# Bias frames built later in program order, and the attention's first loads issued in a forced order

## The chip, the cores and the metric

One core of a Trainium2 chip runs the whole program in one launch. The metric is the device time of one execution in microseconds (us). The core has five instruction streams that each run in order: TensorE (PE, with its weight loads PEld), VectorE (DVE), ScalarE (ACT), GpSimd (POOL) and SyncE (SP, which here only issues DMAs). POOL issues DMAs too. All DMAs share the core's 16 DMA engines.

## What is computed

One layer of a transformer-like backbone over 1024 latent tokens (a 16 x 64 grid) and 256 context tokens, width 1024, fp32. One input projection feeds eight attention heads of size 64 and a long-convolution group of 512 channels; both are normalised, projected out together, and a gated feed-forward layer follows.

```python
def _layer(x, mods, attend, ...):
    h = _rmsnorm(x, norm1_g) * (1.0 + sc1) + sh1
    proj = h @ w_in
    q, k, v = _heads(...), _heads(...), _heads(...)
    hy = _dwconv3(proj[..., 3 * ATTN_WIDTH:], hy_conv_w, hy_conv_b)
    a = attend(q, k, v)                       # latent: neighbourhood attention
    hyo = _hyena(hy, k_f, filt_bias)          # two FFT convolutions with implicit filters
    merged = jnp.concatenate([_rmsnorm(a, ...), _rmsnorm(hyo, ...)], axis=-1)
    x = x + g1 * (merged @ w_out)
    ...                                       # conv feed-forward layer
# neighbourhood attention, per head: an 8 x 16 window with a learned relative bias, plus all context keys
bias = rpb[:, dr[:, None, :, None], dc[None, :, None, :]]
s_loc = jnp.where(col_in, einsum(qg, k_band) * scale + bias, NEG)
s_ctx = einsum(qg, k_ctx) * scale
p = softmax(concatenate([s_loc, s_ctx], -1))
o = einsum(p_loc, v_band) + einsum(p_ctx, v_ctx)
```

## The kernel before

The program is written as straight Python; a list scheduler then sets the order of each engine's stream, from the written order, from priorities and from what it thinks is ready. `tc.issue_after(x)` forces the DMAs (or other instructions) written under it behind instruction x. Stages, in order of time:

- **Projections.** After the first normalisation, `hy_chunk` (L653 and following) makes the long convolution's inputs and `qkv(j, which)` makes Q, K and V of head pair j, all with three-part fp32 matmuls into the banks `psp` (`mm3`, L116 to L118). Results go to DRAM scratch `qd`, `kd`, `vd`. The implicit filters (`filters`, L375 to L489) run beside them and write their spectra to `Kd`, `Kc`.
- **Bias frames.** `rpb_frames(t, var)` (L549 to L558) makes on POOL, for each of three column variants, a frame of the relative bias: a memset, 16 small DMAs, a copy, and a DMA to DRAM scratch `rpw`. Its tile borrows the buffer `fo` of the hyena chunks.
- **Chain.** `chain(j)` is the long convolution of channel group j (five of them, in two interleaved lanes): forward DFT on PE (L805), twiddles on ACT and DVE (L817 to L819), butterflies on DVE (L826 to L831), product with the spectrum `K` loaded from `Kd` on SP (L840 to L847; one buffer `K` per lane), the inverse (L852 to L864, L877), and the gates (L882 to L890). Its inputs `s` are loaded from `lxd` on SP (L791), its result goes to `hyd` (L895, L898). The first phases start in the projections and the rest are interleaved with the attention.
- **Attention.** `attend(p_)` for head pairs 0 to 3. Scores go to `psS` on PE (L1058); DVE adds the bias from `tb0`, `tb1`, `tb2` and takes the maximum (L1079, L1086, L1089); ACT takes exponentials (L1092, L1093); PE transposes (L1102, `psX`), ACT and DVE copy (`pt`, L1006, L1008), PE multiplies with V (L1016, `psav`), and DVE scales into `at` (L1129, L1149). Of all its loads POOL is the issuer: `q` and `k` (L972, L974), `vs` (L1044, L1046: V and cached V), and 16 DMAs of 32 KB for each of the three bias tables of a pair (`bias_load`, L967, from `rpw`). Before pair 0, POOL also fills the three tables with the mask value (L979) and zeroes the borders of the eight probability tiles `Pl` (L984, L985).
- **Output projection** (`wor` loads L1195, splits L1187 and L1188, `token_scales` L1212 to L1226, then matmuls into `psd`), **feed-forward**, final norm. The nine `wor` loads can start only when the chain's pool is given back, which is when its last `hyd` store has landed.

The attention's tiles lie where the projection's operands and weights lay, so each first write waits until the old reader is done. `tb0`, `q0` and `k0` lie in space that is free earlier than that of `Pl`, `tb1` and `tb2`.

Of the kernel before, what the change touches and what calls it, by code (L numbers as in the profile page):

```python
# [11 lines left out]
F32 = mybir.dt.float32  # L12
# [7 lines left out]
P = 128  # L20
# [4 lines left out]
NH, DH = 8, 64  # L25
# [4 lines left out]
NEG = -1e30  # L30
# [47 lines left out]
def build(tc, I, O, dbg=None, upto=99):  # L78
    nc = tc.nc
    V, A, G, T, Q = nc.vector, nc.scalar, nc.gpsimd, nc.tensor, nc.sync  # L80
    dbg = dbg or {}
    top = ExitStack()
    with top:
        _build(nc, tc, top, V, A, G, T, Q, I, O, dbg, upto)


def _build(nc, tc, top, V, A, G, T, Q, I, O, dbg, upto):
    def pool(es, name, bufs=1, **kw):
        return es.enter_context(tc.tile_pool(name=name, bufs=bufs, **kw))
# [51 lines left out]
    def tw_ctx(h):  # L141
# [33 lines left out]
    ld = [("norm1_g", 0, 0, 8), ("norm2_g", 0, 8, 8), ("grp_norm_g", 0, 16, 8), ("hy_conv_w", 0, 40, 36),  # L175
          ("hy_conv_b", 0, 76, 12)]
# [105 lines left out]
    def ft(shape, tag, dt=F32, bufs=1):  # L282
        return fp.tile(shape, dt, tag=tag, name=tag, bufs=bufs)
# [216 lines left out]
    with ies:  # L500
# [3 lines left out]
        for gi, (s, col, tl) in enumerate(groups):  # L504
            xs = []
            for i in tl:
                src, row, _ = tiles[i]
                x = wp.tile([P, D], F32, tag="wada", name="x", bufs=4) if gi in XW else \
# [21 lines left out]
            n = P * len(tl)  # L530
# [19 lines left out]
    def rpb_frames(t, var):  # L550
        f, g = t[:, 0:480], t[:, 512:992]
        G.memset(f, NEG)
        fv = f.rearrange("p (r c) -> p r c", c=32)
        for cq in range(16):
            a = (8 + max(cq - 8, 0), cq, min(cq, 8))[var]
            G.dma_start(out=fv[cq * 8:cq * 8 + 8, :, a:a + 16], in_=I["rpb"][0][:, :, a + 7 - cq:a + 23 - cq])
        G.tensor_copy(g.rearrange("p (u r c) -> p r u c", u=4, r=15), f.rearrange("p (r u c) -> p r u c", u=4, r=15))
        G.dma_start(out=rpw[var].rearrange("q h u x -> (q h) (u x)"), in_=g)  # L558
# [19 lines left out]
    vd = dr.tile([10, P, 512], F32, name="vd")  # L578
# [103 lines left out]
    def qkv(p_, which):  # L682


        w_ = 16 if which == 0 else 8
        t = ip.tile([P, LT], F32, tag=f"cv{turn_('cv')}", name="qkv", bufs=1)

        def sink(ps, c0, n):
            if c0 < LL:
                r0 = c0 // GW  # L690
                src = ps.rearrange("p (r u c) -> p r u c", r=n // GW, c=w_)
                A.copy(t[:, 0:LL].rearrange("p (u r c) -> p r u c", r=16, c=w_)[:, r0:r0 + n // GW], src)
            else:
                A.copy(t[:, LL:LT], ps)

        proj(win[:, :, which * 512 + p_ * P:which * 512 + (p_ + 1) * P], sink, DH ** -0.5 if which == 0 else 1.0)
        if which < 2:
            Q.dma_start(out=(qd, kd)[which][p_, :, 0:LT], in_=t)
        if which == 0:
            return  # L700
        ctx = t[:, LL:LT]
        ps = bk("tB")
        for i in range(2):
            T.transpose(ps[:, i * P:(i + 1) * P], ctx[:, i * P:(i + 1) * P], ident)
        pv = ps[:, 0:256].rearrange("p (n c) -> p n c", n=2)
        so = ip.tile([P, 2, P], F32, tag="st", name="so", bufs=2)
        A.copy(so, pv)
        for i in range(2):
            Q.dma_start(out=O[1 + which][0, 0, 2 * p_:2 * p_ + 2, i * P:(i + 1) * P].rearrange("h t d -> t h d"),
                        in_=so[:, i].rearrange("p (h d) -> p h d", h=2))  # L710
        if which == 2:
            vstore(so, 8, 2, p_)
            for g in range(2):
                ps = bk("tB")
                for i in range(4):
                    T.transpose(ps[:, i * P:(i + 1) * P], t[:, (4 * g + i) * P:(4 * g + i + 1) * P], ident)
                vt = ip.tile([P, 4, P], F32, tag="st", name="vt", bufs=2)
                A.copy(vt, ps.rearrange("p (n c) -> p n c", n=4))
                vstore(vt, 4 * g, 4, p_)
# [4 lines left out]
    def cached(p_):  # L724

        ck = ip.tile([P, 2, P], F32, tag="st", name="ck", bufs=2)
        for h in range(2):
            Q.dma_start(out=ck[:, :, h * DH:(h + 1) * DH],
                        in_=I["cache_ctx_k"][0, 0, 2 * p_ + h].rearrange("(n p) d -> p n d", p=P))
        ps = bk("tB")  # L730
        for i in range(2):
            T.transpose(ps[:, i * P:(i + 1) * P], ck[:, i], ident)
        kt = ip.tile([P, 256], F32, tag="st", name="kt", bufs=2)
        A.copy(kt, ps[:, 0:256])
        Q.dma_start(out=kd[p_, :, LT:], in_=kt)

    for j in range(4):
        for which in range(3):
            hy_chunk(which, j)
            if j + which == 0:  # L740

                t = ft([P, 512], "tm", bufs=2)
# [8 lines left out]
    for j in range(4):  # L751
        for which in range(3):
            if j + which > 0:
                qkv(j, which)
            if j == 0:
                rpb_frames(ip.tile([P, LT], F32, tag="fo", name="rp", bufs=1), which)
        cached(j)
    fes.close()
# [178 lines left out]
    tp = pool(es, "att", reuse_waits="tile")  # L937
# [3 lines left out]
    Pring = [[tp.tile([P, 2, b - a, 16, 8], F32, name=f"Pl{h}{i}") for i, (a, b) in enumerate(BLK)] for h in range(2)]  # L941

    tbs = [None] + [tp.tile([P, NROW * 64], F32, name=f"tb{v}") for v in (1, 2)]
# [12 lines left out]
    blast = [None]  # L956

    def bias_load(p_, var):

        for half in range(2):  # L960
            for rq in range(8):
                r = 8 * half + rq
                r0 = min(max(r - 4, 0), 8)
                nr = HALF_ROWS[half][1]
                a, d = r0 - HALF_ROWS[half][0], r0 - r + 7
                tv = tbs[var][rq * 16:(rq + 1) * 16, HOFF[half]:HOFF[half] + nr * 64].rearrange("q (u x) -> q u x", u=8)
                blast[0] = G.dma_start(out=tv[:, :, a * 8:a * 8 + 64], in_=rpw[  # L967
                    var, :, 2 * p_:2 * p_ + 2, :, d * 8:d * 8 + 64].rearrange("q h u x -> q (h u) x")).ins

    def qkload(p_):  # L970
        q = tp.tile([P, LT], F32, tag=f"q{p_ % 2}", name="q", bufs=1)
        G.dma_start(out=q, in_=qd[p_])  # L972
        k = tp.tile([P, LT + 256], F32, tag=f"k{p_ % 2}", name="k", bufs=1)
        G.dma_start(out=k, in_=kd[p_])  # L974
        return q, k

    first = qkload(0)
    for var in range(3):
        G.memset(tbs[var], NEG)  # L979
        bias_load(0, var)  # L980
        if var == 0:
            for r in Pring:
                for t in r:
                    G.memset(t[:, 0, :, 11:16], 0.0)  # L984
                    G.memset(t[:, 1, :, 0:4], 0.0)  # L985
    blast0 = blast[0]

    sel = tp.tile([P, 4, P], F32, name="sel")
# [49 lines left out]
    def attend(p_):  # L1038

        with tc.issue_after(blast0) if p_ == 1 else ExitStack():  # L1040
            q, k = qkload(p_) if p_ else first
        vs = tp.tile([P, 12, P], F32, tag="vs", name="vs", bufs=2)
        with tc.issue_after(blast0) if p_ == 1 else ExitStack():
            G.dma_start(out=vs[:, 0:10], in_=vd[:, :, p_ * P:(p_ + 1) * P].rearrange("n p x -> p n x"))  # L1044
            for h in range(2):
                G.dma_start(out=vs[:, 10:12, h * DH:(h + 1) * DH],  # L1046
                            in_=I["cache_ctx_v"][0, 0, 2 * p_ + h].rearrange("(n p) d -> p n d", p=P))
        if p_:
            with tc.issue_after(blast0):
                for var in range(3):  # L1050
# [109 lines left out]
    for p_ in range(4):  # L1160
        for n, _ in enumerate(attend(p_)):
            phases(2 - n % 2)
        phases(2)
# [409 lines left out]
    for f in range(NFF):  # L1573
# [8 lines left out]
        t = fpl.tile([P, 2, 2, 256], F32, tag="wt", name="wt", bufs=1)  # L1582
# [191 lines left out]
    for j in range(5):  # L1774
        for i, (g, w) in enumerate(cs):
            dmm(ps[j], g, w, j, False, i == NT - 1)
        t = dp2.tile([P, 512], F32, tag="fx", name="t", bufs=3)
# [44 lines left out]
```

## Time and profile before

| | |
|---|---|
| median of 3 runs | 1855.13 us (1854.43 to 1856.17) |
| the profiled execution's own time | 1859.47 us |
| its span in the trace | 1857.7 us |
| mean granted TensorE clock | 0.962 |
| busy, share of span | PE 93%, PEld 78%, DVE 74%, ACT 48%, POOL 21% |

The profiled execution is 4.3 us (0.23%) longer than the median of the timed runs; the trace's times are its own, from the start of its span. The shares are means over the whole program. The change lies in the stretch from 540 to 880 us, where the projections end, the attention begins, and PE is less busy than in the mean.

### The profile page before, as it was taken

Reading aid. Unit: us, or ns where it says so; the run is one execution under the profiler, and the core shown is the slowest. Engines: PE = TensorE matmul, PEld = TensorE weight load, DVE = VectorE, ACT = ScalarE, POOL = GpSimd, SP = SyncE. Lnnn points to the kernel's source line nnn. Section 1 sums busy time; section 2 is a strip of 40 time slices with the busy share of each in tenths; the row PEclk is TensorE's granted clock in tenths of the full one; section 3 lists DMA queues with packets and bytes.
Section 4 is the critical chain, followed back from the end, with each engine's and each line's share of the span. In section 5 each row is a group of like instructions: output and inputs, shape, how many; then the busy total and the mean of one; then the engine's idle time right before and its main releaser. Section 6 shows DMA issues by size and latency. Waiting matters only on the chain.

```text
span 1857.7 us, 27350 instructions
## 1 busy us (share of the span) xinstructions
PE 1723.9 (93%) x9999; PEld 1453.9 (78%) x9999; DVE 1368.3 (74%) x2166; ACT 892.5 (48%) x1852; POOL 396.3 (21%) x487
## 2 busy tenths in 40 slices
PE   5899999999994689897998899999999999999997
PEld 1688778788783355465886899999999999788786
DVE  4668957861878789873467888889777877556797
ACT  4755545533333576664555444444444444443452
POOL 2366656673018325500110000000000000000001
PEclk7999999999996799898998999999999999999999
DMA  7424354356445323514331444555222122934653
GB/s 265 146 75 142 112 168 131 110 149 211 145 137 160 102 80 102 140 44 144 119 106 65 147 157 146 172 176 165 76 68 67 56 74 96 342 120 136 205 189 130
DMA packets 202438, 249.76 MB, mean 134 GB/s; under 512 B 21922, under 2 KB 147987, under 8 KB 202049
## 3 DMA queue, kind: packets, MB, share of 16 engines
q1 hardware_dynamic: 190360, 230.75, 38.5%
q0 software_dynamic: 10240, 16.46, 3.7%
q8 instruction: 78, 1.28, 0.3%
q10 hardware_dynamic: 1705, 0.82, 0.2%
q14 instruction: 55, 0.45, 0.1%
HBM read 176.75 MB, written 71.20 MB: 133 GB/s over the span
## 4 chain that ended last, share of the span: by engine, by line
PE 54%; DVE 19%; DMA 13%; ACT 5%; issue 5%; POOL 3%; SPq 0%; DVEq 0%; ACTq 0%; POOLq 0%
PE psd L116 5%; PE psd L117 5%; PE psd L118 5%; PE psp L116 4%; PE psp L118 4%; PE psp L117 4%; DMA wt<-in_w_down_dram 3%; PE psa L116 2%; PE psa L117 2%; PE psa L118 2%; DMA tdr<-wt 2%; PE psc L118 2%; PE psc L117 2%; PE psc L116 2%; PE psb L117 1%
## 5 line engine op out<-in xcount | busy, mean ns | idle before, releaser
L116 PE MATMUL psp<-hh,wh 128*128 128x512 f32 (+1 forms) x552 | 200.7, 364 | 1.9 <-ACT wh L121 1.9
L117 PE MATMUL psp<-hl,wh 128*128 128x512 f32 (+1 forms) x552 | 199.0, 361 | 0.0
L118 PE MATMUL psp<-hh,wl 128*128 128x512 f32 (+1 forms) x552 | 199.0, 361 | 0.0
L1737 POOL TENSOR_TENSOR rs<-rs,mhalf 128x1 f32<-128x1 f32 x10 | 7.7, 775 | 816.4 <-DVE rs L1736 816.4
L116 PE MATMUL psa<-T,ws 128*128 128x256 f32 (+1 forms) x528 | 165.8, 314 | 3.8 <-ACT rows L1536 2.7
L117 PE MATMUL psa<-T,ws 128*128 128x256 f32 (+1 forms) x528 | 165.1, 313 | 0.0
L118 PE MATMUL psa<-T,ws 128*128 128x256 f32 (+1 forms) x528 | 164.6, 312 | 0.0
L116 PE MATMUL psd<-wd,gs 128*128 128x512 f32 x360 | 140.7, 392 | 3.6 <-ACT gs L121 3.6
L117 PE MATMUL psd<-wd,gs 128*128 128x512 f32 x360 | 141.0, 392 | 0.0
L118 PE MATMUL psd<-wd,gs 128*128 128x512 f32 x360 | 123.8, 391 | 2.0 <-DVE gs L122 2.0
L116 PEld LDWEIGHTS psp<-hh,wh 128*128 128x128 f32 x552 | 104.9, 190 | 23.2 <-issue 7.4
L118 PEld LDWEIGHTS psp<-hh,wl 128*128 128x128 f32 x552 | 104.6, 189 | 15.3 <-issue 1.2
L117 PEld LDWEIGHTS psp<-hl,wh 128*128 128x128 f32 x552 | 104.9, 190 | 14.0 <-issue 0.4
L116 PE MATMUL psc<-T,ws 128*128 128x384 f32 (+1 forms) x352 | 110.0, 313 | 6.0 <-ACT ws L121 6.0
L967 POOL DMA_DIRECT2D tb<-rpw x192 | 100.3, 530 | 58.0 <-DVE m L1079 24.3
L117 PE MATMUL psc<-T,ws 128*128 128x384 f32 (+1 forms) x352 | 110.1, 313 | 0.0
L118 PE MATMUL psc<-T,ws 128*128 128x384 f32 (+1 forms) x352 | 109.7, 312 | 0.0
L117 PE MATMUL psb<-T,ws 128*128 128x384 f32 (+1 forms) x352 | 109.4, 311 | 0.0
L118 PE MATMUL psb<-T,ws 128*128 128x384 f32 (+1 forms) x352 | 109.4, 311 | 0.0
L116 PE MATMUL psb<-T,ws 128*128 128x384 f32 (+1 forms) x352 | 109.2, 310 | 0.0
L116 PEld LDWEIGHTS psa<-T,ws 128*128 128x128 f32 x528 | 101.3, 192 | 5.5 <-ACT rows L1536 3.9
L117 PEld LDWEIGHTS psa<-T,ws 128*128 128x128 f32 x528 | 101.3, 192 | 0.0
(404 smaller groups left out, 4783.9 us busy)
## 6 DMA issues: line engine op xcount, KB each, us to landing
wada<-in_w_ada_dram SPq DMA_DIRECT2D x48, 512.0 KB
wr<-in_w_up_dram SPq DMA_DIRECT2D x44, 512.0 KB
gr<-gdr SPq DMA_DIRECT2D x44, 320.0 KB
wr<-in_w_in_dram SPq DMA_DIRECT2D x23, 512.0 KB
wt<-in_w_down_dram SPq DMA_DIRECT2D x44, 256.0 KB
tdr<-wt SPq DMA_DIRECT2D x44, 256.0 KB
gdr<-cv SPq DMA_DIRECT2D x22, 512.0 KB
wr<-tdr SPq DMA_DIRECT2D x20, 512.0 KB
```

The source lines that it names most:

```text
L116: T.matmul(out, ah, bh, start=start, stop=False, skip_group_check=True)
L117: T.matmul(out, ah, bl, start=False, stop=False, skip_group_check=True)
L118: T.matmul(out, al, bh, start=False, stop=stop, skip_group_check=True)
L967: blast[0] = G.dma_start(out=tv[:, :, a * 8:a * 8 + 64], in_=rpw[var, :, 2 * p_:2 * p_ + 2, :, d * 8:d * 8 + 64].rearrange("q h u x -> q ( ...
L1737: G.tensor_tensor(rs, rs, mhalf, op=ALU.pow)
```

## The change

Two edits. First, the three `rpb_frames` calls move in written order from head pair 0 to head pair 2 of the `qkv` loop. Second, the loads ahead of the attention get a forced order on POOL: the fill and the 16 loads of `tb0` first, then the three `vs` loads of pair 0 (a new helper `vload`), then, behind `vs`, the border memsets of `Pl`, and the fills and loads of `tb1` and `tb2`. Nothing is computed otherwise; the number of instructions on each engine is the same.

```diff
-            if j == 0:
+            if j == 2:
                 rpb_frames(ip.tile([P, LT], F32, tag="fo", name="rp", bufs=1), which)
...
+    def vload(p_):
+        vs = tp.tile([P, 12, P], F32, tag="vs", name="vs", bufs=2)
+        G.dma_start(out=vs[:, 0:10], in_=vd[:, :, p_ * P:(p_ + 1) * P].rearrange("n p x -> p n x"))
+        for h in range(2):
+            ld = G.dma_start(out=vs[:, 10:12, h * DH:(h + 1) * DH],
+                             in_=I["cache_ctx_v"][0, 0, 2 * p_ + h].rearrange("(n p) d -> p n d", p=P))
+        return vs, ld.ins
...
     first = qkload(0)
-    for var in range(3):
-        G.memset(tbs[var], NEG)
-        bias_load(0, var)
-        if var == 0:
-            for r in Pring:
-                for t in r:
-                    G.memset(t[:, 0, :, 11:16], 0.0)
-                    G.memset(t[:, 1, :, 0:4], 0.0)
+    G.memset(tbs[0], NEG)
+    bias_load(0, 0)
+    with tc.issue_after(blast[0]):
+        vfirst, vlast = vload(0)
+    with tc.issue_after(vlast):
+        for r in Pring:
+            for t in r:
+                G.memset(t[:, 0, :, 11:16], 0.0)
+                G.memset(t[:, 1, :, 0:4], 0.0)
+        for var in (1, 2):
+            G.memset(tbs[var], NEG)
+            with tc.issue_after(blast[0]):
+                bias_load(0, var)
...
-        vs = tp.tile([P, 12, P], F32, tag="vs", name="vs", bufs=2)
         with tc.issue_after(blast0) if p_ == 1 else ExitStack():
-            G.dma_start(out=vs[:, 0:10], in_=vd[:, :, p_ * P:(p_ + 1) * P].rearrange("n p x -> p n x"))
-            for h in range(2):
-                G.dma_start(out=vs[:, 10:12, h * DH:(h + 1) * DH],
-                            in_=I["cache_ctx_v"][0, 0, 2 * p_ + h].rearrange("(n p) d -> p n d", p=P))
+            vs = vload(p_)[0] if p_ else vfirst
```

**POOL, at the frames** (`rp` is a frame's tile, `cs0` and `GO` are the filters' tiles; difference of the order before and after). This is where the moved calls stand in the stream:

```order
 L395 TENSOR_TENSOR cs0_2317<-sd11_2315,sd01_2308 128x512
-L552 MEMSET rp_4064 128x480
-L556 DMA rp_4064<-in_rpb_dram 8x15x16 x13
+L552 MEMSET rp_4714 128x480
+L556 DMA rp_4714<-in_rpb_dram 8x15x16 x13
 L455 TENSOR_TENSOR GO_2068<-GO_2068 128x2x2x128
```

Only the tile's number differs: the frames stand between the same two filter instructions as before, and so do the two other frames. Up to the attention's first loads, the streams of all five engines are the same, instruction by instruction and with the same semaphore waits.

**POOL, ahead of head pair 0, before** (with the semaphores that each waits for):

```order
L979 MEMSET tb0_5857 128x1472 [waits DMAHW1_49,PE_49,Activation_49]
L984 MEMSET Pl00_5833 128x3x40 [waits PE_49]
...
L967 DMA tb0_5857<-rpw_723 16x8x64 [waits Pool_49]
...
L979 MEMSET tb1_5841 128x1472
L979 MEMSET tb2_5842 128x1472
L1044 DMA vs_5944<-vd_728 128x10x128 [waits DMASW5_49]
L1046 DMA vs_5944<-in_cache_ctx_v_dram 128x2x64 [waits DMASW6_49]
```

and after:

```order
L987 MEMSET tb0_5857 128x1472 [waits DMAHW1_49,PE_49,Activation_49]
L967 DMA tb0_5857<-rpw_723 16x8x64 [waits Pool_49]
...
L972 DMA vs_5879<-vd_728 128x10x128 [waits DMASW5_49,PE_49]
L974 DMA vs_5879<-in_cache_ctx_v_dram 128x2x64 [waits DMASW6_49]
...
L994 MEMSET Pl00_5833 128x3x40
...
L997 MEMSET tb1_5841 128x1472
L997 MEMSET tb2_5842 128x1472
```

The wait for PE that the first `Pl` memset had is now the first `vs` load's, on the same semaphore value (the last projection matmul into `psp`). The 16 `tb0` loads now stand ahead of that wait, and no instruction was added.

**DVE, at the end of the attention, before** (`L890` is the chain's last instruction on DVE, `L1188` the split of an output weight, `at` the attention's result, `ria` the token scales):

```order
L890 TENSOR_TENSOR s_8075<-s_8075,s_8073 128x2x256
L1139 TENSOR_TENSOR l<-l,l_8098 128x8
L1182 COPY sh_8287<-mods 128x16
L1024 RECIPROCAL lrow_5941<-l 128x4 x2
...
L1188 SCALAR_TENSOR_TENSOR wl_8328<-wor,vec,wh_8327 128x512
L1149 TENSOR_TENSOR at_5828<-psav,bs 128x2x16x16
L1220 TENSOR_SCALAR ria<-psX 128x2
```

and after:

```order
L890 TENSOR_TENSOR s_8075<-s_8075,s_8073 128x2x256
L1159 TENSOR_TENSOR at_5828<-psav,bs 128x2x16x16
L1020 COPY pt<-psX 128x512
...
L1198 SCALAR_TENSOR_TENSOR wl_8304<-wor,vec,wh_8303 128x1024
L1159 TENSOR_TENSOR at_5828<-psav,bs 128x2x16x16
L1230 TENSOR_SCALAR ria<-psX 128x2
```

The scheduler interleaves chain and attention differently from the second score block of pair 0 on, on PE, DVE and ACT. At the end, 134 attention matmuls stood on PE behind the chain's last matmul before, and 86 do now. Eight of the nine weight splits stood ahead of the attention's last write to `at` before; four do now.

## Rows read from the trace of the kernel before

**Rows 1.** By stretch: length, busy PE, PEld, DVE, ACT, POOL; clock, DMA share, GB/s

```profile
560.00:600.00 40.00, 20.50 (x68) 14.91 (x68) 33.51 (x58) 16.33 (x56) 33.84 (x72) 0.63 0.58 153
...
620.00:834.00 214.00, 188.79 (x1133) 115.53 (x1131) 176.79 (x391) 136.58 (x439) 73.82 (x138) 0.95 0.31 82
834.00:878.00 44.00, 34.38 (x213) 23.36 (x213) 17.16 (x28) 21.88 (x40) 2.37 (x2) 0.88 0.39 122
```

**Rows 2.** Chain that ended last, 538 to 660: start, us, what

```profile
562.24 8.32 POOL tb L967 x16
...
573.49 8.39 DMA vs<-vd
...
582.16 6.13 DMA tb<-rpw
...
602.58 7.93 DMA K<-Kd
```

**Rows 3.** Timeline of DVE: start, us, instruction, [idle before <-releaser]

```profile
585.75 0.48 DVE L819 SCALAR_TENSOR_TENSOR s<-pscA,tw,t 128x256 f32<-128x256 f32 x1 [3.58 <-ACT t L818]
...
597.77 0.42 DVE L1079 CUSTOM_DVE_ANT_0 Pl<-psS,tb 128x264 f32<-128x264 f32 x1
...
605.69 1.21 DVE L1086 TENSOR_REDUCE n<-psS 128x4 f32<-128x1024 f32 x1
610.60 1.23 DVE L844 TENSOR_TENSOR s<-s,K 128x1024 f32<-128x1024 f32 x1 [3.69 <-DMA K<-Kd]
```

**Rows 4.** Timeline of POOL ahead of head pair 0

```profile
544.20 1.33 POOL L979 MEMSET tb<- 128x1472 f32 x1 [3.60 <-PE pstB L704]
560.26 0.20 POOL L984 MEMSET Pl<- 128x120 f32 x1 [14.73 <-PE psp L118]
...
562.18 8.38 POOL L967 DMA_DIRECT2D tb<-rpw  x16
...
573.49 0.98 POOL L1044 DMA_DIRECT2D vs<-vd  x1
574.46 1.44 POOL L1046 DMA_DIRECT2D vs<-in_cache_ctx_v_dram  x2
...
582.16 4.17 POOL L967 DMA_DIRECT2D tb<-rpw  x8 [3.65 <-DMA vs<-vd]
588.58 9.89 POOL L967 DMA_DIRECT2D tb<-rpw  x19 [2.25 <-DMA tb<-rpw]
598.46 0.57 POOL L972 DMA_DIRECT2D q<-qd  x1
```

**Rows 5.** Chain that ended last, 480 to 700: an earlier load of K

```profile
502.56 3.73 DMA K<-Kd
```

**Rows 6.** Timelines of SP and of PE at one load of s

```profile
574.54 0.37 SPq L791 DMA_DIRECT2D s<-lxd  x1
...
582.72 6.25 PE L805 MATMUL pscA<-s,dftf 128*128 128x256 f32 x16 [9.09 <-DMA s<-lxd]
```

**Rows 7.** Timeline at the end of the attention: PE, DVE and SP

```profile
829.28 1.89 PE L877 MATMUL pscA<-s,idft 128*128 128x256 f32 x8
839.59 0.65 PE L1016 MATMUL psav<-pt,vs 128*64 128x256 f32 x4
840.17 0.66 PE L1102 MATMUL psX<-ident,Pl 128*128 128x128 f32 x4
877.16 0.77 PE L116 MATMUL psd<-w,ar 128*128 128x512 f32 x1
...
833.27 0.68 DVE L890 TENSOR_TENSOR s<-s,s 128x512 f32<-128x512 f32 x1
862.14 0.74 DVE L1188 SCALAR_TENSOR_TENSOR wl<-wor,vec,wh 128x512 fp32r<-128x512 f32 x1
864.68 0.69 DVE L1149 TENSOR_TENSOR at<-psav,bs 128x512 f32<-128x512 f32 x1 [1.79 <-ACT bs L1033]
...
836.83 26.41 SPq L1195 DMA_DIRECT2D wor<-in_w_out_dram  x9
```

## The prediction

> **What bounds the kernel now.** I read the busy time by stretch first, since the shares of the whole program say nothing about the place of the change. From 560 to 600 us, where the attention starts, no engine is full: DVE is busy 33.5 of 40 us, PE 20.5 at a granted clock of 0.63, POOL 33.8. From 620 to 834 us PE is busy 188.8 and DVE 176.8 of 214 us, so both are close to the limit. In the last stretch, 834 to 878, DVE is busy 17.2 of 44 us: the work waits on itself there [rows 1]. Outside 540 to 880 us the change alters nothing that I can find, apart from one swap of two neighbouring DMAs on SP in the feed-forward.
>
> Next I read the chain of waits. It goes through POOL: 16 loads of `tb0` (8.32 us), the landing of `vs` (8.39), the landing of a bias load (6.13) [rows 2]. Taken at its word, 22.8 us of POOL's loading lie on the path. The timeline of DVE says otherwise. The first instruction that needs `tb0` is L1079 at 597.77, and it shows no idle time ahead of it: DVE came to it straight from the chain's butterflies [rows 3]. The last `tb0` load was issued by 570.56 (562.18 + 8.38) [rows 4], 27 us earlier. The chain view followed a wait for many semaphores and picked the wrong one. So the tables of pair 0 are not late, and what counts is only the idle time that DVE and PE do show: 3.58 us of DVE ahead of 585.75, where PE had waited 9.09 us for a load of `s`, and 3.69 us of DVE ahead of 610.60, waiting for `K` [rows 3, 6].
>
> **The frames.** The first edit moves nothing. The order shows the frames between the same filter instructions, with the same waits, on POOL and on all other engines. Cost 0, with no range.
>
> **POOL ahead of pair 0.** Before, `tb0` is filled at 544.20, then POOL stands 14.73 us behind the first `Pl` memset until the last projection matmul ends at 560.2. Then come memsets, 16 loads, memsets, `vs` at 573.49, and 32 loads with 5.90 us of waits between them (3.65 for `vs`, 2.25 for a bias load), until `q` of pair 1 is issued at 598.46 [rows 4]. After the change the 16 loads (8.38 us) fill the 14.73 us hole: they run from 545.5 to about 554. Then `vs` waits, since it took over the wait for PE, until 560.2, and its three issues take 2.4 us (0.98 + 1.44). Sixteen border memsets cost about 2.4 us (thirteen took 560.26 to 562.18, less than 0.15 us each), two fills 2 x 1.33, 32 loads 32 x 0.524 = 16.8 us. That is 560.2 + 2.4 + 2.4 + 2.7 + 16.8 = 584.5 for `q` of pair 1 if the loads find no wait, and 590.4 if they find all the 5.90 us again. So POOL runs 8 to 14 us ahead. By itself this is worth nothing, since nothing waited for the tables.
>
> **What it is worth (term 1).** The load of `K` issued at 602.58 took 7.93 us to land [rows 2]. An earlier one took 3.73 [rows 5]. Between 598.46 and 602 POOL had issued `q`, `k` and `vs` of pair 1 in one burst [rows 4], so the slow one shared the DMA engines with it. When the burst is issued at 584.5 to 590.4 instead, it has landed before 602.58 even if it takes the 8.4 us that `vs` took [rows 2]. `K` then lands at 602.58 + 3.73 = 606.3; DVE is busy until 605.69 + 1.21 = 606.9, and the 3.69 us of idle time are gone. ACT's exponentials of pair 0 come behind that DVE work, so they move too. I take the whole 3.69 us. Lower bound of the gain 0, if the 16 loads of `tb0` for pair 1, which may now follow at once, slow `K` just as much.
>
> **Term 2, the load of `s` at 574.54** [rows 6]. `vs` leaves its window (it was issued at 573.49), but more bias loads enter it: before, POOL was still at the memsets until 573.49, after it issues a bias load every 0.52 us from about 567.7. The Trainium skill, page DMA: Bandwidth & Descriptors, section Issuing engines are not separate DMA queues, says that DMAs of all issuers run on the same 16 DMA engines and interleave; the trace agrees at the `K` load (7.93 us beside 3.73). By that rule the bias loads from POOL take from this load about what `vs` gives back. Gain bounds: 3.58 us (all of DVE's idle time) and -2 us (7.93 - 3.73 = 4.2 is the price of a full burst, and the bias loads come half as dense). I take 0.
>
> **Term 3, the end of the attention.** The scheduler, which thinks the tables come earlier, now places attention ahead of chain work. Total work is equal, but the tail differs. Before, the chain's last DVE instruction ends at C = 833.95, the first output matmul `psd` starts at 877.16, 43.2 us later; 134 attention matmuls stood behind the chain, and attention's last write to `at` began at 864.68 [rows 7]. Now 86 stand behind it. Then attention ends about 86/134 of (865.4 - 834.0 = 31.4 us), 20.2 us, after the new C', and the first `psd` follows by the old distance of 877.2 - 865.4 = 11.8: C' + 32.0. The other condition is the weight splits: the nine `wor` loads start only behind C, at 836.83, and the eighth split ends at 862.9, C + 28.9 [rows 7]; the token scales now stand behind it on DVE, and take some 3 us more: C' + 32. Both give 11.2 us less than 43.2. But C' is later, since 48 more attention matmuls stand ahead of it. An attention pair of groups, two `psav` matmuls (four records) and four transposes, takes 0.58 us for the first and as long for the second [rows 7], 0.195 us for each of the six; 48 cost 9.4 us of PE. PE is busy 88% of that stretch [rows 1], so nothing hides all of it; C' is 9.4 us later if PE sets the pace and some 3.5 if DVE does (five fewer rows, three copies of about 0.68 us among them), and at most 9.4/0.88 = 10.7, or 15 with a new stall of 4 us. I take 10, near PE's row: gain 11.2 - 10 = 1.2 us, between 7.7 and -3.8.
>
> **The sum.** 3.7 + 0 + 1.2 = 4.9 us. Against the profiled execution's own time, 1859.47, that gives 1854.6; the timed runs' median was 1855.13, so I forecast 1855.1 - 4.9 = 1850.2 us. A measurement of this kernel can tell about 0.2%, 3.7 us, from no change.
>
> **The rivals.**
> *The chain of waits is right* (chance 0.10). Then the tables did hold DVE up, and 14 us of POOL's time (598.46 - 584.5) come off: 1841. For it: the pieces of the chain [rows 2]; against it: no idle time ahead of L1079 [rows 3].
> *It is taken up again* (0.29). PE at 88% and DVE at 83% from 620 on [rows 1] leave little room, the bias tables of later pairs wait for the same DVE instructions as before, and 3.7 us at one place are absorbed or term 1 is halved: 1852 to 1858, within 0.2%.
> *The chain falls behind* (0.19, the other side). The nine `wor` loads hang on the chain's end and take 26.4 us [rows 7]. Attention first means chain last. Of C' later by x, term 3 gives 11.2 - x, so with term 1 it turns into a loss from x = 14.9 on. Each microsecond beyond costs one; slower by over 0.2% from x = 18.6 on, or from x = 14.9 if term 1 is gone, since in-order streams that now hold chain instructions behind attention ones can stall: 1859 to 1863.
> *The forecast's case* (0.42): 1843 to 1851.
>
> **How the numbers follow.** Faster by over 0.2%: forecast and first rival, 0.52. Same: 0.29. Slower: 0.19. The forecast's own range is 1843 to 1851 (terms 1 and 3 with their best bounds give 3.7 + 7.7 = 11.4; term 2 could add 3.6). The range over all cases, 1842 to 1860, leaves out the first rival and the worst of the third.
>
> **What would show it.** `tb0` loads at 545 to 554 and no hole of 14.7 us in front of `Pl`, but one of about 6 us in front of `vs`. `q` of pair 1 issued by 590. `K` of the load near 602 landing in under 5 us, and DVE without the wait of 3.7 us. The first `psd` matmul at 871 to 873 rather than 877.2 in the trace. I am wrong if that `K` load still takes 8 us, if DVE shows idle time ahead of L1079 now, or if the `wor` splits end more than 3 us behind attention's end plus 8 us.

## The result and the profile after

The changed kernel took 1843.59 us (median of 4 runs, 1842.62 to 1844.07) beside 1855.16 us (4 runs, 1854.43 to 1856.17) for the kernel before: ratio 0.9937, 95% interval 0.9919 to 0.9954. That is 11.7 us faster (8.5 to 15.0), where 4.9 us were forecast; 1843.6 lies in the range 1842 to 1860, at the edge of the forecast's own case (1843 to 1851).

The profiled execution took 1843.86 us, span 1841.9. Its times can't be laid on those of before directly, since it starts late: the fill of `tb0`, ahead of which nothing was changed, stands at 548.54 instead of 544.20 [rows 4]. Below I count from that fill. POOL's timeline after (start, us, instruction, [idle before <-releaser]; the lines named below have the numbers of before up to L967 and are 8 to 18 higher behind it; `vs` is now loaded in the helper `vload`, L972 and L974):

```profile
548.54 1.33 POOL L987 MEMSET tb<- 128x1472 f32 x1 [3.59 <-PE pstB L704]
550.17 8.40 POOL L967 DMA_DIRECT2D tb<-rpw  x16 [0.30 <-POOL tb L987]
564.69 0.98 POOL L972 DMA_DIRECT2D vs<-vd  x1 [6.12 <-issue]
...
589.51 2.61 POOL L967 DMA_DIRECT2D tb<-rpw  x5 [2.26 <-DMA tb<-rpw]
592.15 0.57 POOL L980 DMA_DIRECT2D q<-qd  x1
```

The 16 loads of `tb0` lie in the former hole, 6.12 us of it are left in front of `vs`, and `q` of pair 1 is issued 43.6 us behind the fill instead of 54.3 [rows 4].

The two loads of terms 1 and 2, on SP:

```profile
577.37 0.37 SPq L791 DMA_DIRECT2D s<-lxd  x1
...
602.88 7.07 SPq L840 DMA_DIRECT2D K<-Kd  x2
```

and what uses them on DVE, and the attention's first instruction that needs `tb0`:

```profile
586.11 0.48 DVE L819 SCALAR_TENSOR_TENSOR s<-pscA,tw,t 128x256 f32<-128x256 f32 x1 [0.22 <-ACT t L818]
...
597.47 0.69 DVE L831 TENSOR_TENSOR s<-s 128x512 f32<-128x512 f32 x1
598.07 0.42 DVE L1089 CUSTOM_DVE_ANT_0 Pl<-psS,tb 128x264 f32<-128x264 f32 x1
...
606.53 0.68 DVE L890 TENSOR_TENSOR s<-s,s 128x512 f32<-128x512 f32 x1
607.24 1.23 DVE L844 TENSOR_TENSOR s<-s,K 128x1024 f32<-128x1024 f32 x1
```

The idle 3.69 us ahead of `K`'s use are gone, and of the 3.58 us ahead of L819 0.22 are left [rows 3]. From the issue of `s` to L819 it is 8.7 us instead of 11.2, from the issue of the first `K` to its use 4.4 instead of 8.0 [rows 2, 3, 6].

The end of the attention, as the chain of waits after (start, us, what):

```profile
827.60 0.70 DVE s L890
828.32 2.78 DMA hyd<-s
...
831.17 3.40 DMA wor<-in_w_out_dram
...
856.72 0.75 DVE wl L1198
...
857.50 2.51 DMA wor<-in_w_out_dram
860.01 0.02 issue
860.04 0.72 ACT wh L1197
860.76 0.52 ACT ar L1291
861.27 0.04 issue
861.32 0.79 PE psd L116
```

The chain ends at C' = 828.29 and the first `psd` follows 33.0 us behind it, instead of 43.2 [rows 7]. It now waits for the ninth `wor` load: ACT scales that weight (L1197) before it writes `ar`. On DVE the last write to `at` ended 14.3 us ahead of the ninth split's end:

```profile
846.55 0.69 DVE L1159 TENSOR_TENSOR at<-psav,bs 128x512 f32<-128x512 f32 x1 [0.75 <-ACT bs L1047]
...
860.79 0.75 DVE L1198 SCALAR_TENSOR_TENSOR wl<-wor,vec,wh 128x512 fp32r<-128x512 f32 x1 [0.40 <-ACT wh L1197]
```

What the stretch is made of shows best when it is cut at `K`'s use and at the chain's end. The columns are those of [rows 1]; first before, then after:

```profile
610.60:833.95 223.35, 191.31 (x1138) 116.89 (x1138) 186.16 (x405) 141.29 (x457) 76.82 (x144) 0.93 0.32 88
833.95:877.16 43.21, 33.59 (x213) 22.63 (x211) 16.51 (x27) 21.93 (x40) 2.37 (x2) 0.89 0.38 119
```

```profile
607.24:828.29 221.05, 200.06 (x1202) 120.53 (x1200) 187.77 (x410) 147.59 (x474) 74.83 (x140) 0.95 0.32 88
828.29:861.32 33.03, 25.34 (x155) 18.38 (x154) 15.04 (x23) 16.28 (x23) 2.38 (x2) 0.82 0.48 158
```

In the mixed stretch PE does 64 more instructions, 8.75 us of work, and DVE 1.6 us more, and yet the stretch is 2.3 us *shorter*. The difference is small but it repeats: in the experiments below the stretch took 222.6 to 223.4 us in the three traces with the order of before and 219.7 to 221.6 in the four with the new order. From the fill to the first `psd` the trace went from 332.96 to 312.78 us: 7.7 up to `K`'s use, 2.3 in the mixed stretch, 10.2 behind the chain.

### The profile page after: what moved, and what is told of

Same layout as the page of the kernel before. It is cut to its first block, busy times and chain, and to the rows that moved or that the text cites. A ratio compares the mean times of both kernels' runs of the same rounds, so it can differ in the third digit from the quotient of the medians.

```text
span 1841.9 us, 27359 instructions
## 1 busy us (share of the span) xinstructions
PE 1725.3 (94%) x9999; PEld 1453.2 (79%) x9999; DVE 1367.1 (74%) x2166; ACT 893.9 (49%) x1852; POOL 396.7 (22%) x487
## 4 chain that ended last, share of the span: by engine, by line
PE 38%; DVE 14%; DMA 8%; issue 4%; ACT 3%; POOL 1%; DVEq 0%; POOLq 0%; ACTq 0%; SPq 0%
PE psd L116 6%; PE psd L117 6%; PE psd L118 6%; PE psa L116 3%; PE psa L117 3%; PE psa L118 3%; DMA wt<-in_w_down_dram 2%; PE psc L118 2%; PE psc L117 2%; PE psc L116 2%; PE psb L117 2%; PE psb L118 2%; PE psb L116 2%; DMA tdr<-wt 2%; POOL tb L967 1%
## 5 line engine op out<-in xcount | busy, mean ns | idle before, releaser
L117 PEld LDWEIGHTS psp<-hl,wh 128*128 128x128 f32 x552 | 104.8, 190 | 14.1 <-issue 0.4
L967 POOL DMA_DIRECT2D tb<-rpw x192 | 100.5, 531 | 45.1 <-DVE m L1089 31.7
```

What stands on the lines that cost most here:

```text
L117: T.matmul(out, ah, bl, start=False, stop=False, skip_group_check=True)
```

## The experiments

Two theories were set against each other. **A:** the earlier loads themselves pay, by freeing the DMA engines for `s` and `K`. **B:** the order pays, in which the scheduler now writes attention and chain on PE, DVE and ACT. The table gives, for each kernel's trace, the time from the fill of `tb0` to `K`'s use, from there to the chain's end, from there to the first `psd`, and the ratio of timed runs to the kernel before with its 95% interval. Each number is a difference of two rows as above (for before 610.60 - 544.20 = 66.4).

| kernel | to K's use | to chain's end | to psd | sum | ratio |
|---|---|---|---|---|---|
| before | 66.4 | 223.4 | 43.2 | 333.0 | |
| changed | 58.7 | 221.1 | 33.0 | 312.8 | 0.9937 (0.9919 to 0.9954) |
| frames alone | 66.9 | 223.0 | 43.1 | 332.9 | 0.9995 (0.9983 to 1.0007) |
| loads alone | 60.1 | 220.7 | 32.6 | 313.5 | 0.9924 (0.9898 to 0.9949) |
| vs first, tables late | 64.1 | 224.1 | 44.3 | 332.5 | 1.0003 (0.9990 to 1.0016) |
| vs behind fills | 59.7 | 221.6 | 33.0 | 314.3 | 0.9936 (0.9919 to 0.9952) |
| old loads, new order | 65.6 | 219.7 | 32.9 | 318.2 | 0.9951 (0.9931 to 0.9971) |
| new loads, old order | 59.7 | 222.6 | 43.2 | 325.5 | 0.9997 (0.9981 to 1.0013) |
| changed, chain faster | 61.3 | 221.8 | 39.4 | 322.5 | 0.9960 (0.9947 to 0.9974) |
| before, chain faster | 63.6 | 215.2 | 57.8 | 336.5 | 1.0051 (1.0034 to 1.0069) |
| tables late, third order | 63.8 | 228.1 | 35.4 | 327.4 | 0.9988 (0.9972 to 1.0004) |
| more PE | 61.8 | 226.7 | 32.8 | 321.4 | 0.9945 (0.9928 to 0.9962) |
| more DVE | 59.6 | 228.8 | 32.7 | 321.1 | 0.9984 (0.9969 to 1.0000) |
| four wor buffers | 61.4 | 220.5 | 29.9 | 311.8 | 0.9917 (0.9889 to 0.9944) |

**The two edits apart.** Frames alone:

```diff
-            if j == 0:
+            if j == 2:
                 rpb_frames(...)
```

> Only the first edit: the bias frames are made at the third head pair instead of the first; the attention's loads stand as before. The order of all five engines is that of the kernel before. Theory A (the earlier loads themselves free the DMA engines for K and s): 1855.2, within 1.5 us. Theory B (the time comes from the new order in which attention and chain stand on PE, DVE and ACT): 1855.2 as well. A rival, that the frames matter after all, expects 1851 or less. Its trace is also a second look at the kernel before: the profiled execution of before was 4.3 us above its median, and this one shows where.

Loads alone is the changed kernel with that line as before. So are the pinned kernels new loads, old order, more PE and more DVE further down: they have the changed loads, but not the first edit.

> Only the second edit: the attention's loads as in the changed kernel, the bias frames at the first head pair as before. All five engines have the order of the changed kernel. Both theories: 12 us below the kernel before, as the changed kernel; from the fill of tb0 to the first psd 312.8 us as in the changed kernel's trace, within 2. If the frames pay in company of the loads: 5 us less gain.

Both came as expected: 0.9995 and 0.9924. No run shows the frames to be worth anything, alone or in company. A second trace of either stream repeats the sum of the first within 0.8 us, and the single columns within 1.5. The 4.3 us by which the profiled execution of before exceeds its median don't show in this stretch: frames alone, profiled at its own median, has the same 332.9 us.

**The load of vs.** vs first, tables late:

```diff
     with tc.issue_after(blast[0]):
-        vfirst, vlast = vload(0)
-    with tc.issue_after(vlast):
         for r in Pring:
...
-            vs = vload(p_)[0] if p_ else vfirst
+            vs = vload(p_)[0]
```

> The loads of vs stand ahead of the tables' loads on POOL, and these behind vs: vs is issued when the projection's last matmul ends, as in the changed kernel, the 16 loads of tb0 start only then, as in the kernel before. PE, ACT and SP have the order of the kernel before, DVE all but eight rows. Theory A: vs no longer meets the load of s, and pair 1's burst is out before the load of K near 602: 3.4 + 3.7 = 7 us less than before, 1848, with 43 us from the chain's end to the first psd as before. Theory B: the order is the old one, so 1855 within 2.

Measured: 1.0003, no change. The trace shows half of what A said. `vs` left the load of `s` alone (8.4 us from its issue to L819, as after), but POOL was no earlier, and pair 1's burst met `K` again:

```profile
600.90 0.57 POOL L980 DMA_DIRECT2D q<-qd  x1
```

```profile
602.12 0.32 SPq L840 DMA_DIRECT2D K<-Kd  x1
```

```profile
609.99 1.22 DVE L844 TENSOR_TENSOR s<-s,K 128x1024 f32<-128x1024 f32 x1 [3.54 <-DMA K<-Kd]
```

The 2.3 us won up to `K`'s use were gone by the first `psd` (332.5 against 333.0), with the old order of PE and ACT.

vs behind fills is the changed kernel with `vs` issued behind the border memsets and the two fills:

```diff
-                G.memset(t[:, 1, :, 0:4], 0.0)
+                border = G.memset(t[:, 1, :, 0:4], 0.0)
...
+    def vload_0():
+        with tc.issue_after(border.ins):
+            return vload(0)[0]
...
-            vs = vload(p_)[0] if p_ else vfirst
+            vs = vload(p_)[0] if p_ else vload_0()
```

> The changed kernel with vs of pair 0 issued behind the border memsets and the two fills, some 5 us later; PE, DVE, ACT and SP have the changed kernel's order word for word. Theory A: vs meets the load of s again for part of its way, and up to 2 us of DVE's idle time come back: 1844 to 1846. Theory B: 1843.6, within 1 us.

0.9936, as the changed kernel. From the issue of `s` to L819 it took 8.6 us, though DVE stood idle there for 2.41 us: `s` was issued 29.8 us behind the fill, after the change 28.8. It tells nothing between the theories. But it shows that the forced place of `vs` isn't what brings the new order: the four other streams kept it.

**Loads and order crossed.** Since the scheduler answers a load with another order, both change together in any edit of the source. So I took the order of the instructions on PE, DVE, ACT and SP from the one program and forced it on the other, with edges that order instructions of one engine and add no wait (POOL, which issues the loads, was left as it was):

```diff
+def pin(tc, nc):
+    own = {}
+    for i in nc.cur_bb.bb.instructions:
+        if type(i).__name__.startswith("Inst"):
+            own.setdefault(str(i.engine).split(".")[-1], []).append(i)
+    info = mybir.DependencyInfo(mybir.DependencyClass.NoSync, mybir.DependencyReason.DATA)
+    for engine, stretches in STREAMS.items():
+        for text in stretches:
...
+            for x, y in zip(at, at[1:]):
+                tc.add_manual_dep(own[engine][y], own[engine][x].name, info, reason="pin")
```

`STREAMS` holds for each engine the numbers of its instructions, as written, in the order wanted. `at` is that list.

> The kernel before with its own first loads on POOL (tb0 behind the hole, vs late, pair 1's burst near 600), but PE, DVE, ACT and SP pinned by added order edges to the streams of the changed kernel, instruction for instruction. Theory A (the early loads pay): the load of K near 602 takes 8 us again and the kernel is as before, within 2 us. Theory B (the order pays): the chain ends at 223 us or less behind that K's use, the first psd follows it by 33 us instead of 43, and the kernel is 7 to 12 us below the kernel before.

> The other half: the changed kernel's first loads on POOL, but PE, DVE, ACT and SP pinned to the streams of the kernel before. Theory A: K lands in 4 to 5 us, its use is some 6 us earlier against the last projection matmul, and this stays: 5 to 7 us below the kernel before. Theory B: what is won there is mostly given back by the end of the attention, where the first psd again comes 43 us behind the chain's end: within 3 us of the kernel before.

Old loads, new order: 0.9951, 9.1 us faster (5.4 to 12.8), though `K` was as slow as ever (600.98 to 608.74, DVE idle 3.43 us). The use of `K`, and its two stretches:

```profile
608.74 1.23 DVE L949 TENSOR_TENSOR s<-s,K 128x1024 f32<-128x1024 f32 x1 [3.43 <-DMA K<-Kd]
```

```profile
608.74:828.41 219.67, 198.54 (x1197) 119.29 (x1197) 187.61 (x410) 147.58 (x473) 77.95 (x146) 0.95 0.33 90
828.41:861.29 32.88, 25.44 (x154) 18.46 (x153) 15.03 (x23) 16.15 (x23) 2.37 (x2) 0.81 0.50 157
```

New loads, old order: 0.9997, 0.6 us faster (3.5 faster to 2.4 slower), though `K` was used 4.3 us after its issue:

```profile
603.46:826.04 222.58, 191.74 (x1143) 116.65 (x1142) 186.09 (x406) 141.93 (x458) 75.38 (x142) 0.94 0.32 88
826.04:869.27 43.23, 33.65 (x213) 22.62 (x211) 16.57 (x27) 22.01 (x40) 2.37 (x2) 0.89 0.37 120
```

Each pair of lines is close to that of the kernel whose order it has. Theory A falls as the main cause, B stands: the order carries most of the gain, and the loads by themselves none that the runs could tell. Whether the loads add something once the new order is there stays open: without them the ratio was 0.9951, with them 0.9937, 0.9924 and 0.9936, and these intervals overlap.

**How much attention stands behind the chain.** The same edit was made to the changed kernel and to the kernel before:

```diff
         for n, _ in enumerate(attend(p_)):
-            phases(2 - n % 2)
+            phases(3 - n % 2)
```

> The changed kernel's loads, but with three phases of the chain ahead of each first half of a pair instead of two: 134 attention matmuls stand behind the chain's last, as in the kernel before, where the changed kernel has 86. The first 390 attention matmuls stand as in the changed kernel. Theory A: the gain up to 610 us stays, the tail is again some 43 us behind the chain's end, and the chain ends some 9 us earlier: 1844, within 2. Theory B: 1851 to 1855, since the old tail is back.

> The kernel before, loads and all, with three phases of the chain ahead of each first half of a pair instead of two: 180 attention matmuls stand behind the chain's last, 46 more than before. Theory A: the loads are the old ones, so same as before within 2 us. Theory B: the chain ends no earlier for it, since not the attention's matmuls set its pace, and the first psd comes 46 x 0.234 = 11 us later behind it: 6 to 11 us slower than before. If the chain ends earlier by what stands behind it now (46 x 0.195 = 9 us), as the prediction's term 3 has it: 2 us slower at most.

And a third order came from issuing `vs`, then the borders, then the tables:

```diff
-    G.memset(tbs[0], NEG)
-    bias_load(0, 0)
-    with tc.issue_after(blast[0]):
+    fill = G.memset(tbs[0], NEG)
+    with tc.issue_after(fill.ins):
         vfirst, vlast = vload(0)
...
-                G.memset(t[:, 1, :, 0:4], 0.0)
+                border = G.memset(t[:, 1, :, 0:4], 0.0)
+        with tc.issue_after(border.ins):
+            bias_load(0, 0)
```

> The loads of vs first, then the border memsets, and the 16 loads of tb0 only behind these: POOL is as late as in the kernel before. The scheduler writes yet another order, with 86 attention matmuls behind the chain's last, as in the changed kernel. Theory A (the tables and the burst of pair 1 must be early): same as before within 2 us, above all the load of K near 602 slow again. Theory B (what counts is how much attention stands behind the chain's end): some 33 us from the chain's end to the first psd instead of 43, 10 us less than before in the trace, 6 to 10 in the timed runs.

Changed, chain faster: 0.9960, 7.4 us faster, between the two expectations. The chain ended no earlier (221.8 against 221.1) though 48 attention matmuls fewer stood ahead of its end; the first `psd` came 6.4 us later behind it. Before, chain faster: 1.0051, 9.5 us slower. The size is B's, the way isn't: the chain did end 8.2 us earlier, as the prediction's price per matmul had it, but the tail grew by 14.6. The rows of that kernel:

```profile
612.12:827.28 215.16, 182.96 (x1065) 110.60 (x1065) 178.35 (x383) 129.47 (x419) 77.11 (x145) 0.92 0.34 91
827.28:885.06 57.78, 45.08 (x287) 29.34 (x284) 25.65 (x49) 33.20 (x78) 2.37 (x2) 0.91 0.28 90
```

So 46 attention matmuls, with their DVE and ACT work, took 0.18 us each in the mixed stretch and 0.32 in the tail. Tables late, third order: 0.9988, not to be told from before. The tail was short (35.4), as B said, but the mixed stretch had grown by 4.8 us. B in the form "only the tail counts" fails here: an order has to be good in both stretches.

**What a microsecond costs in the mixed stretch.** In both kernels the streams, POOL's too, are pinned to those of the changed kernel, and the added instructions are left out of the pinning. The pinned kernel without them was not run; old loads, new order (0.9951) is the nearest on the same chip.

```diff
             ps = bk("X")
-            for h in range(2):
-                for i in range(2):
-                    T.transpose(ps[:, (2 * h + i) * P:(2 * h + i + 1) * P], src(h, i), ident)
+            turn.n += 1
+            for more in ((True, False) if p_ in (1, 2) and turn.n % 3 == 0 else (False,)):
+                for h in range(2):
+                    for i in range(2):
+                        t = T.transpose(ps[:, (2 * h + i) * P:(2 * h + i + 1) * P], src(h, i), ident)
+                        if more:
+                            EXTRA.add(t.ins.name)
...
         if evict.i % 3 == 0:
+            if now[0] in (1, 2):
+                EXTRA.add(V.tensor_copy(t, ps).ins.name)
             V.tensor_copy(t, ps)
```

(the first piece is more PE, the second more DVE).

> The changed kernel with its streams pinned, and 16 times four transposes of pairs 1 and 2 done twice: 64 more PE instructions, 64 x 0.146 = 9.3 us of PE's time in the stretch of chain and attention, nothing more on any other engine. If PE sets the pace of that stretch, as the prediction's term 3 took it: the chain ends 8 to 10 us later and the kernel is only 3 to 5 us below the kernel before. If DVE sets it and PE's work falls into PE's idle time: the chain's end moves by less than 2.5 us and the kernel stays 10 to 13 us below the kernel before.

> The changed kernel with its streams pinned, and 16 copies of DVE in pairs 1 and 2 done twice: 16 x 0.60 = 9.6 us more of DVE's time in the same stretch, nothing more on PE. If PE sets the pace: the chain's end moves by less than 3 us. If DVE sets it: the chain ends 7 to 10 us later, and the kernel is only 2 to 6 us below the kernel before.

```profile
609.49:836.20 226.71, 204.74 (x1266) 126.33 (x1264) 187.92 (x411) 147.49 (x474) 74.69 (x140) 0.97 0.31 86
```

```profile
608.27:837.03 228.76, 199.59 (x1202) 120.07 (x1200) 197.77 (x426) 148.12 (x474) 74.63 (x140) 0.96 0.31 85
```

More DVE: 10.0 us more of DVE's time (197.77 against 187.77) made the stretch 7.7 us longer, and the kernel fell back to 0.9984; as expected if DVE sets the pace. More PE: 64 more instructions made it 5.7 us longer in the trace. They were expected to be 9.3 us of PE's time, but PE's busy time rose by 4.7 (204.74 against 200.06, with the granted clock at 0.97 against 0.95). In the timed runs no loss shows (0.9945; 10.2 us below before, 7.1 to 13.4). The trace lies between the two expectations, the runs lie where DVE sets the pace. So DVE's price shows in both, and PE's only in one trace.

**Four wor buffers.** The end of the chain of waits after pointed to the `wor` loads:

```diff
-        parts = [(slice(0, D), ("wh7", "wl7")[k % 2])] if k < 7 else [(slice(c, c + 512), "ot") for c in (0, 512)]
+        parts = [(slice(0, D), ("wh7", "wl7", "wh6", "wl6")[k % 4] if k < 6 else "wh7")] if k < 7 else [(slice(c, c + 512), "ot") for c in (0, 512)]
```

> The changed kernel, where the first wor loads go round four buffers instead of two. In the changed kernel's trace the last split of the first eight ends 33.3 us behind the chain's end, the attention's last write to at 19.0, and the first psd follows the split at once. If the wor loads set the first psd: it comes 2 to 4 us earlier, 11 to 12 us behind the attention's end; the kernel is 2 to 4 us faster than the changed one, 14 to 16 below the kernel before. If the attention's end sets it: no change, 12 below the kernel before.

The nine loads were issued within 20.87 us instead of 26.66, and the first `psd`, at 857.28, follows the attention's last write to `at` by 12.0 us instead of the ninth load:

```profile
830.23 20.87 SPq L1205 DMA_DIRECT2D wor<-in_w_out_dram  x9
```

```profile
844.61 0.68 DVE L1159 TENSOR_TENSOR at<-psav,bs 128x512 f32<-128x512 f32 x1
```

```profile
857.28 0.77 PE L116 MATMUL psd<-w,ar 128*128 128x512 f32 x1
```

That is 29.9 us behind the chain's end, 3.1 less than after. The runs gave 0.9917, 15.4 us below before (10.4 to 20.6) and the lowest median here, 1839.38, beside 1842.77 for loads alone on the same chip. The intervals of the two overlap, so that 3 us more were won is shown in the trace and only likely in the runs.

## Why the prediction was right and where it was wrong

**Frames, and POOL ahead of pair 0.** Right: the frames are worth nothing that the runs show (0.9995), and the loads lie as worked out, less the 4.3 us of late start: `tb0` 545.8 to 554.2, `q` of pair 1 at 587.8, 10.7 us ahead of before, between the bounds of 8 and 14. DVE came to L1089 without idle time, as it did to L1079 before, so the chain of waits was indeed followed to the wrong wait. The rival that took it at its word (1841) names nearly the time that came, but its mechanism is refuted: with the new loads and the old order nothing was gained.

**Term 1.** The mechanism and its size in the trace were right: 3.7 us of idle time gone. What the idle time was worth is another matter (below). Over the fourteen traces `K` was used 4.2 to 4.6 us after its issue where `q` of pair 1 had been issued at least 9.8 us ahead of it, and 7.8 to 8.2 us where it was at most 4.1 us ahead.

**Term 2.** Taken as 0, it was 2.5 us in the trace. The three kernels that leave `vs` late took 10.2 to 11.9 us from the issue of `s` to L819, as does the one with old loads and new order (11.2); the ten with `vs` early 8.3 to 9.3. The bias loads that took the place of `vs` cost far less than it. By the Trainium skill, page DMA: Bandwidth & Descriptors, section Issuing engines are not separate DMA queues, DMAs of all issuers interleave on the same 16 engines, so the bias loads had to be expected to take part of what `vs` gave back. The trace doesn't contradict that they share the engines, but the net was 2.5 us, not 0.

**The worth of terms 1 and 2.** Here the sum was too high. With the old order the two gave 0.6 us in the timed runs (3.5 faster to 2.4 slower), where 3.7 were booked. The rival "it is taken up again" describes this part. Where it is taken up isn't settled: the trace of that kernel still holds 7.5 us at the first `psd`, but its profiled execution (1852.31) was the fastest of its twelve runs, and that of before lay 4.3 us above its median.

**Term 3 is the step that failed.** Its distance was right: C' + 33.0 against C' + 32.0 (the eighth split at C' + 29.2, where C' + 32 was given; the ninth load, which the prediction didn't count, set the end). What was wrong is "C' is 10 us later, near PE's row". PE did get 8.75 us more work ahead of the chain's end, as its row said, and C' didn't move back for it: the mixed stretch became 2.3 us shorter, in the pinned kernel with the old loads 3.7. The price was taken from busy times, and the argument was that PE is busy 88% of that stretch, so that nothing hides all of it. But 32 us of PE's time were idle there (223.35 - 191.31), and with the new order 21 are left (221.05 - 200.06). Work added where it happens to stand can cost: 64 more PE instructions, as many as the new order moved here, made the stretch 5.7 us longer in the trace, and 10.0 us more of DVE 7.7. The price per matmul itself came true once: before, chain faster took 46 matmuls out of the stretch and its chain ended 8.2 us earlier, where the price says 9; changed, chain faster took out 48 and its chain ended no earlier. So an order can't be priced by an engine's sum. Which waits the new order fills was not followed instruction by instruction. Term 3 with its true size is 10.2 + 2.3 = 12.5 us in the trace, outside its bounds of 7.7 to -3.8. In the runs that had the order alone it is 9.1 us (5.4 to 12.8), well above the 1.2 that were booked; that interval still reaches into the bounds. The rival on the other side, that the chain falls behind, hung on the same step: it needed C' 14.9 us later.

**That the range held is in part luck.** Of the 4.9 us, 3.7 were booked for the loads, which gave 0.6 by themselves, and 1.2 for the order, which gave 9.1. The two errors go opposite ways. With both terms at their best bounds the sum was 11.4 us, and 11.7 came.

**What would have shown it.** Of the signs named, `tb0`, the hole, `q` and `K` came as said. The first `psd` was forecast for 871 to 873; it came at 861.32, or 857.0 less the late start. Of the three marks for a wrong prediction two didn't occur: `K` was not slow, and DVE had no idle time ahead of L1089. The third, the `wor` splits ending later than 858.2 (the attention's end at 847.24, plus 8, plus 3), was missed barely by the eighth split, at 857.47, on which the prediction's sum rests. By the ninth, at 861.5, it did occur, and the ninth load is what the first `psd` waited for.

**What stays open.** The traces show more than the runs. From the fill to the first `psd` the changed kernel gained 20.2 us and loads alone 19.5, where the runs gave 11.7 (8.5 to 15.0) and 14.1 (9.5 to 18.9). About 1.9 us of it belongs to the end of the projections: from the fill to their last matmul it took 14.1 us in six traces, the changed kernel's among them, and 15.9 to 16.3 in the others, whatever their edits. The first 540 us, in which the streams are alike, varied as well: that matmul ended at 560.2 in the trace of before, 562.7 in that of after, and between 557.9 and 563.7 over all. One trace for each kernel can't tell whether the rest is chance or a cost that the change has elsewhere.

## What to carry to other kernels

When a list scheduler writes the streams, an edit of a few loads is two edits: what the loads do on the chip, and the order with which the scheduler answers. Take the orders from the built programs, count what stands behind the last instruction of the longest chain, and, where it matters which of the two pays, pin the streams of the one program onto the other. Price moved work by where it goes: into idle time of its engine beside other work it can be free (8.75 us of PE here) but need not be (46 attention matmuls were worth 0.18 us each there in the other order), and at the end of the stage the same 46 cost 0.32 us each.

## What was not expected of the hardware

A burst of 32 KB bias loads, one each 0.52 us, disturbed a load of `s` far less than the one transfer of 640 KB that they replaced (8.3 to 9.3 us to its use against 10.2 to 11.9). And the load of `K` fell into two groups, 4.2 to 4.6 and 7.8 to 8.2 us to its use, with nothing between; but in no trace did pair 1's burst lead it by 4.2 to 9.8 us, so that a smooth passage isn't excluded.
